# An interleave of two tensors: which part of each tensor makes up one tile, 4 MiB on end or the same 32 KiB of every partition

## The chip, the cores and the metric

The kernel runs on one core of one Trainium2 chip. The metric is the device time of one execution in microseconds (us). The time before the change is 314.18 us, the median of 3 runs (314.18 to 314.37).

## The reference

Two float32 tensors of 32 x 256 x 1024 elements (32 MiB each) are woven element by element into one of 32 x 256 x 2048 (64 MiB).

```python
batch, seq, dim = 32, 256, 1024
result = np.zeros((batch, seq, dim * 2), dtype=np.float32)
result[..., 0::2] = x
result[..., 1::2] = y
```

Seen flat, element i of x goes to place 2i and element i of y to place 2i + 1. So any cut of x and y into pieces at the same places gives pieces of the output that can be made apart from each other.

## The kernel before, in words

The flat tensors are cut into n = 8 tiles. A tile is 128 partitions x 8192 float32 (32 KiB of each partition, 4 MiB) of x and of y, and 128 x 16384 (64 KiB of each partition, 8 MiB) of the output. The helper `rows` makes the view of tile k: before the change it takes the k-th run of 4 MiB (8 MiB of the output) on end and gives each partition the next 32 KiB (64 KiB) of it. So rows that stand under each other in a tile's DMA start 32 KiB apart in x and y, and 64 KiB apart in the output.

In SBUF there are two buffers each for x (`xt`), y (`yt`) and the output (`ot`). An output buffer holds half a tile's output: 128 partitions x 8192 float32, 32 KiB a partition. Three queues work:

- SP issues all loads in order: x of tile 0 as two halves (lines 42 and 43), then for each tile x (line 50) and y (line 53). From tile 2 on it waits until VectorE has read the buffer that the load overwrites.
- VectorE (DVE) goes through tiles and halves. For each half, a copy puts 4096 elements of x in the even places of `ot` (line 67), and one puts 4096 of y in the odd places (line 70). From tile 1 on it waits before the first of them until the last store from that output buffer has landed.
- ACT issues the stores, each 4 MiB, when both copies of a half are done (line 83). The very first store is cut in two, of 8 KiB and of 24 KiB of each partition (lines 77 and 81).

Loads and stores are on queues of their own, q1 (loads, from SP) and q10 (stores, from ACT), and both are worked off by the same 16 DMA engines. The last of a DMA's 16 increments of its semaphore comes when all of its rows have landed. The first two loads are put ahead of a barrier at the program's start by the last lines of `tile_interleave_kernel`.

Of the kernel before, what the change touches and what calls it, by code (L numbers as in the profile page):

```python
# [3 lines left out]


def _interleave(nc, x, y, out):
    P = 128
    W = 8192
    H = W // 2  # L10

    total = 1
    for s in x.shape:
        total *= s
    n = total // (P * W)
    assert n * P * W == total

    def rows(ap, names, k):
        flat = ap.rearrange("b s d -> (b s d)")
        return flat[k * names : (k + 1) * names].rearrange("(p w) -> p w", p=P)  # L20

    fp32 = mybir.dt.float32
    xt = [nc.alloc_sbuf_tensor(f"xt{b}", [P, W], fp32).ap() for b in (0, 1)]
    yt = [nc.alloc_sbuf_tensor(f"yt{b}", [P, W], fp32).ap() for b in (0, 1)]
    ot = [nc.alloc_sbuf_tensor(f"ot{b}", [P, W], fp32).ap() for b in (0, 1)]

    xsem = [nc.alloc_semaphore(f"xsem{b}") for b in (0, 1)]
    hsem = nc.alloc_semaphore("hsem")
    qsem = nc.alloc_semaphore("qsem")
    ysem = [nc.alloc_semaphore(f"ysem{b}") for b in (0, 1)]  # L30
    woven = nc.alloc_semaphore("woven")
    osem = [nc.alloc_semaphore(f"osem{b}") for b in (0, 1)]


    cuts = [0, W // 4, W]
    parts = [slice(a, b) for a, b in zip(cuts, cuts[1:])]

    xs = [rows(x, P * W, k) for k in range(n)]
    ys = [rows(y, P * W, k) for k in range(n)]
    os_ = [rows(out, 2 * P * W, k) for k in range(n)]  # L40

    nc.sync.dma_start(out=xt[0][:, :H], in_=xs[0][:, :H]).then_inc(xsem[0], 16)
    nc.sync.dma_start(out=xt[0][:, H:], in_=xs[0][:, H:]).then_inc(hsem, 16)

    for k in range(n):
        b = k % 2
        if k >= 2:
            nc.sync.wait_ge(woven, 4 * (k - 2) + 3)
        if k:
            nc.sync.dma_start(out=xt[b], in_=xs[k]).then_inc(xsem[b], 16)  # L50
        if k >= 2:
            nc.sync.wait_ge(woven, 4 * (k - 2) + 4)
        nc.sync.dma_start(out=yt[b], in_=ys[k]).then_inc(ysem[b], 16)

    for k in range(n):
        b = k % 2
        for h in (0, 1):
            c = slice(h * H, (h + 1) * H)
            if h == 0:
                nc.vector.wait_ge(xsem[b], 16 * (k // 2 + 1))  # L60
            elif k == 0:
                nc.vector.wait_ge(hsem, 16)
            if k:
                nc.vector.wait_ge(osem[h], 16 * k)
            if (k, h) == (1, 0):
                nc.vector.wait_ge(qsem, 16)
            nc.vector.tensor_copy(out=ot[h][:, 0::2], in_=xt[b][:, c]).then_inc(woven, 1)  # L67
            if h == 0:
                nc.vector.wait_ge(ysem[b], 16 * (k // 2 + 1))
            nc.vector.tensor_copy(out=ot[h][:, 1::2], in_=yt[b][:, c]).then_inc(woven, 1)  # L70

    for k in range(n):
        for h in (0, 1):
            nc.scalar.wait_ge(woven, 4 * k + 2 * h + 2)
            if (k, h) == (0, 0):
                for c in parts[:-1]:
                    nc.scalar.dma_start(
                        out=os_[k][:, c], in_=ot[h][:, c]
                    ).then_inc(qsem, 16)
                c = parts[-1]  # L80
                nc.scalar.dma_start(out=os_[k][:, c], in_=ot[h][:, c]).then_inc(osem[h], 16)
                continue
            nc.scalar.dma_start(
                out=os_[k][:, h * W : (h + 1) * W], in_=ot[h]
            ).then_inc(osem[h], 16)

    nc.scalar.wait_ge(osem[0], 16 * n)
    used = sorted(s.num for s in [*xsem, hsem, qsem, *ysem, woven, osem[0]])
    assert used == list(range(used[0], used[-1] + 1)), used
    nc.scalar.sem_clear(range(used[0], used[-1] + 1))  # L90
    nc.sync.nop(nofuse=True).wait_op(osem[1], 16 * n, "sem-ge").then_inc(
        osem[1], -16 * n
    )


def kernel(tc, x, y, out):
    nc = tc.nc
    tc.close()
    tc.compile()

    _interleave(nc, x, y, out)

    blocks = nc.main_func.blocks
    for engine in (mybir.EngineType.SP, mybir.EngineType.SP):
        opening = blocks[0].instructions
        at, moved = next(
            (b, i)
            for b in blocks[1:]
            for i in b.instructions
            if i.engine == engine and i.opcode == "DMACopy"  # L110
        )
        assert not (moved.sync_info and moved.sync_info.on_wait)
        body = at.instructions
        body.remove(moved)
        gate = next(
            n
            for n, i in enumerate(opening)
            if i.engine == engine and i.opcode == "Drain"
        )
        opening.insert(gate, moved)  # L120
        at.instructions = body
        blocks[0].instructions = opening


# [1 line left out]
_INS = ['x', 'y']  # L126
_OUTS = [((32, 256, 2048), 'float32')]


# [23 lines left out]
```

## Time and profile before

| What | Value |
|---|---|
| Median of 3 runs | 314.18 us |
| Span of the profiled execution, first to last instruction | 312.9 us |
| Median less span: what lies around the span | 1.3 us |
| VectorE busy | 72.0 us of 312.9 |
| Moved between HBM and SBUF | 67.11 MB read, 67.11 MB written |
| Mean rate over the span | 429 GB/s |
| DMA packets | 4896 in 34 DMAs |
| From issue to landing, median: a store of 4 MiB | 34.1 us |
| From issue to landing, median: y, and x from tile 1 on | 41.5 and 24.3 us |

No total of its own is recorded for the profiled execution beside its span; the median of the runs stands in for it.

How to read it: the profile takes one execution. The DMA part lists each queue with the number of its packets, the MB it moved, and the time that its packets took as a share of 16 engines' span. 100% means that all 16 engines had a packet in hand all the time. The packets of a queue in a stretch, asked for by window, are counted by where they start, and one engine can begin a packet while another's end is still out, so the shares of a short stretch can add up to a little over 100%. Multiplying a share by 16 and by the length of the stretch gives engine time; divided by the MB moved, it is the engine time that one MB cost.

### The profile page before, as it was taken

The page shows a single profiled execution, that of the slowest core. Times are in us where ns is not written, and L with a number is a line of the kernel's source. Part 1 is how long each engine was busy: PE and PEld are TensorE (multiplying, and loading weights), DVE is VectorE, ACT ScalarE, POOL GpSimd, SP SyncE. Part 2 cuts the span into 40 slices and gives each one's busy share as a digit, 9 for nine tenths or more (in the row PEclk, how much of TensorE's full clock was granted, in tenths as well). Part 3 has the DMA queues.
Part 4 walks back from the last instruction along what each step waited for, and adds up shares of the span by engine and source line. Part 5 has one row for each costly group of instructions (what it writes and reads, how often), then busy time and mean ns, then how long its engine had stood idle before and what let it go on. Part 6 is the DMA issues. An engine that isn't in the chain of part 4 may idle for free.

```text
span 312.9 us, 114 instructions
## 1 busy us (share of the span) xinstructions
DVE 72.0 (23%) x32; POOL 0.2 (0%) x4
## 2 busy tenths in 40 slices
DVE  0216000501305023050220503205032050415410
POOL 0000000000000000000000000000000000000000
DMA  8999999999999999999999999999999999999998
GB/s 337 467 402 436 436 402 419 452 457 415 427 444 411 461 402 469 402 469 402 469 402 465 406 440 432 423 448 402 469 402 469 402 469 402 469 402 448 423 423 381
DMA packets 4896, 134.22 MB, mean 429 GB/s; under 512 B 544, under 2 KB 544, under 8 KB 544
## 3 DMA queue, kind: packets, MB, share of 16 engines
q1 hardware_dynamic: 2448, 67.11, 50.1%
q10 hardware_dynamic: 2448, 67.11, 49.7%
HBM read 67.11 MB, written 67.11 MB: 429 GB/s over the span
## 4 chain that ended last, share of the span: by engine, by line
DMA 82%; DVE 12%; issue 0%
DMA out_dram<-ot 76%; DMA yt<-in_y_dram 6%; DVE ot L70 6%; DVE ot L67 6%
## 5 line engine op out<-in xcount | busy, mean ns | idle before, releaser
L67 DVE COPY ot<-xt 128x4096 f32<-128x4096 f32 x16 | 36.7, 2295 | 213.8 <-DMA out_dram<-ot 206.5
L70 DVE COPY ot<-yt 128x4096 f32<-128x4096 f32 x16 | 36.6, 2288 | 12.3 <-DMA yt<-in_y_dram 12.3
L137 POOL MEMSET const-bfloat16-1.0<- 128x1 bf16 x1 | 0.1, 103 | 0.0
L137 POOL MEMSET const-uint8-127<- 128x1 uint8 x1 | 0.1, 102 | 0.0
L137 POOL MEMSET const-float32-0.0<- 128x1 f32 x1 | 0.1, 100 | 0.2 <-issue 0.2
L137 POOL MEMSET const-float32-1.0<- 128x1 f32 x1 | 0.1, 99 | 0.0
## 6 DMA issues: line engine op xcount, KB each, us to landing
out_dram<-ot ACTq DMA_DIRECT2D x15, 4096.0 KB, 34.1
yt<-in_y_dram SPq DMA_DIRECT2D x8, 4096.0 KB, 41.5
xt<-in_x_dram SPq DMA_DIRECT2D x7, 4096.0 KB, 24.3
xt<-in_x_dram SPq DMA_DIRECT2D x2, 2048.0 KB, 9.5
out_dram<-ot ACTq DMA_DIRECT2D x1, 3072.0 KB, 32.8
out_dram<-ot ACTq DMA_DIRECT2D x1, 1024.0 KB, 16.3
```

The costliest lines, as they stand in the source:

```text
L67: nc.vector.tensor_copy(out=ot[h][:, 0::2], in_=xt[b][:, c]).then_inc(woven, 1)
L70: nc.vector.tensor_copy(out=ot[h][:, 1::2], in_=yt[b][:, c]).then_inc(woven, 1)
L137: nc = _bacc.Bacc("TRN2", target_bir_lowering=False, num_devices=1)
```

## The change

One line of the helper `rows` changes. The flat tensor is first divided among the 128 partitions, so that each owns 256 KiB of x and of y (512 KiB of the output) on end, and tile k is the k-th 32 KiB (64 KiB) of each of them. Rows that stand under each other in a DMA now start 256 KiB apart in x and y, and 512 KiB apart in the output. The number of tiles, the DMAs, their sizes, the length of each row, the copies, the waits and their order stay as they are.

```diff
     def rows(ap, names, k):
         flat = ap.rearrange("b s d -> (b s d)")
-        return flat[k * names : (k + 1) * names].rearrange("(p w) -> p w", p=P)
+        return flat.rearrange("(p w) -> p w", p=P)[:, k * names // P : (k + 1) * names // P]
```

## The prediction

> **What bounds the kernel now.** I read the page's busy times first, then its DMA part, then the waits, then a table by stage.
>
> ```profile
> DVE 72.0 (23%) x32; POOL 0.2 (0%) x4
> DMA  8999999999999999999999999999999999999998
> DMA packets 4896, 134.22 MB, mean 429 GB/s; under 512 B 544, under 2 KB 544, under 8 KB 544
> q1 hardware_dynamic: 2448, 67.11, 50.1%
> q10 hardware_dynamic: 2448, 67.11, 49.7%
> ```
>
> VectorE works 23% of the span. The 16 DMA engines are busy in every slice; loads (q1) take 50.1% of their time and stores (q10) 49.7%, together 99.8%. So the span is the sum of all packets' times over 16: 0.998 x 312.9 = 312.3 us.
>
> ```profile
> DVE ot L67 <- DMA out_dram<-ot: 206.5, 14, 29.0
> ```
>
> In the waits, VectorE stands 206.5 us for stores. It has room to be late, the DMA engines have none.
>
> ```profile
> 0.00:28.60 28.60, 8.99 (x4) 0.20 (x4) 1.00 0.97 403
> 28.60:76.80 48.20, 4.50 (x3) 0.00 (x0) 1.00 1.02 435
> 76.80:270.40 193.60, 44.97 (x20) 0.00 (x0) 1.00 1.00 433
> 270.40:312.90 42.50, 13.49 (x6) 0.00 (x0) 1.00 0.97 419
> ```
>
> The table by stage (stretch, length, VectorE and GpSimd busy with counts, clock, DMA share, GB/s) shows the same in each stage: a share of 0.97 to 1.02. There is no stage in which a longer packet would be hidden.
>
> What does a packet cost? The DMA part of the steady stretch from 80 to 270 us, by queue: packets, MB, share.
>
> ```profile
> q1 hardware_dynamic: 1417, 41.19, 50.2%
> q10 hardware_dynamic: 1409, 41.16, 50.2%
> ```
>
> Loads: 0.502 x 16 x 190 us / 41.19 MB = 37.05 us of engine time per MB. Stores: 37.08. A row of 32 KiB (0.0328 MB) takes 1.21 us on its engine. Loads have rows 32 KiB apart, stores 64 KiB apart, and they cost the same within 0.1%: here it is the engine's own pace that sets a packet's time, and memory keeps up.
>
> It doesn't keep up everywhere. The same part for 0 to 7 us, where the first loads run alone:
>
> ```profile
> q1 hardware_dynamic: 160, 2.36, 87.6%
> ```
>
> This is 0.876 x 16 x 7 / 2.36 = 41.6 us per MB, 12% over the steady value. And for 25 to 42 us, where the first stores join the loads:
>
> ```profile
> q1 hardware_dynamic: 181, 5.41, 76.9%
> q10 hardware_dynamic: 160, 1.44, 20.0%
> ```
>
> Loads: 0.769 x 16 x 17 / 5.41 = 38.7, 4.3% over. So a packet can be stretched by what it meets in memory, by 0% in the steady state, by 4.3% and by 12% in two short stretches. Over the whole span the stretched loads cost (50.1% - 49.7%) x 312.9 = 1.25 us.
>
> **The change part by part.**
>
> *Instructions.* None is added, removed or moved: 32 copies of 2.29 us, 34 DMAs, the same waits. Copies work in SBUF alone, whose layout stays. Cost 0, and it needs no cover.
>
> *Issue.* The DRAM side of a load of x from tile 1 on, and of y, was one run of 4 MiB and becomes 128 rows with gaps. An issue of such a load takes 0.327 us on SP now; an issue of a store, whose rows have gaps already, takes 0.339 us on ACT. I cost it at 15 x 0.012 = 0.2 us of SP's time and nothing of the span: from tile 2 on SP sits idle for over 200 us before line 50 (218.1 us in 6 waits), and queued rows keep the engines busy meanwhile. If that cover were gone it would be 0.2 us.
>
> *Number of packets.* Both queues have 2448 packets for 67.11 MB, though before the change loads have one run and stores have gaps. So a packet already is a row (or an increment) in both cases, and the number stays. Cost 0.
>
> *The time of a packet.* This is the whole question. Rows go from 32 to 256 KiB apart (loads) and from 64 to 512 KiB (stores), so the rows that 16 engines work at in one moment are eight times as far apart. The trace before has no such distance, so I bound it. From below: all loads at the pace of the stores, the 1.25 us of stretched loads gone, 312.9 us. From the same side, the one comparison that the trace has (32 against 64 KiB) gives 0. From above: every packet stretched as the loads at 25 to 42 us are, 0.043 x 312.3 = 13.4 us, 327.6 us. The 12% of the first 7 us I don't carry over the whole run: that is a start from rest.
>
> Between 0 and 4.3% I take the middle, 2.15%, and on the stores alone, since their rows come to lie twice as far apart as the loads', the farthest from what the trace shows to be free. Stores take 0.497 x 312.9 = 155.5 us; 0.0215 x 155.5 = 3.3 us. The reason for taking more than the nearest row's 0: with 99.8% of the engines' time in use any stretch at all shows in full, and powers of two this large make many rows differ in few address bits. That is an inference from the layout, not a row.
>
> *The sum.* 0 + 0 + 0 + 3.3 us on a span of 312.9, so 316.2 us; with the 1.3 us by which the median of the runs (314.18) is over the span, **317.5 us**, 1.1% slower.
>
> The Trainium skill speaks against this change: its page "DMA: Bandwidth & Descriptors", section "Latency and other measured facts", lists copies of tiles of 128 rows of 16 KiB between HBM tensors, at 207 GB/s per direction with rows 512 KiB apart, against 214 in full, 164 at 2 MiB and 103 at 4 MiB, and advises laying tiles out contiguously. An estimate from that page, 214/207 on all packets, would make the sum 0.034 x 312.3 = 10.6 us, 324.8 us in all; on stores alone it would be 5.3 us, 319.5 us. The row from which I go, 64 KiB apart at 37.08 us per MB, lies outside what the page lists, and no trace so far shows 256 or 512 KiB.
>
> **The rivals.**
>
> *The engines' pace stays the bound (not slower).* Memory serves rows 256 and 512 KiB apart as fast as it serves 32 and 64; each packet of 32 KiB stays at 1.21 us. For it: two distances with the same cost, and the steady rate is the same with loads alone, both, or stores alone. Against it: the loads at 25 to 42 us, which show that memory can fall short. It decides as long as memory answers a row in less than 1.21 us. 314.2 us, chance 0.22.
>
> *The stretched loads of the opening go (faster).* The opening's 12% and 4.3% could come from rows that stand close together, and rows farther apart could spread better. It decides in the first 42 us only, and can give at most the 1.25 us above: 312.9 us; half of it, 313.6 us. Against it: the same close rows are read at full pace from 80 us on, so a start from rest explains the stretch as well. Chance 0.13.
>
> *Loads and stores both stretch, by 4.3% or more.* Rows meet in the same part of memory in every tile, both ways: 327.6 us if as at 25 to 42 us. For it: the engines work at their rows in step (equal packets, equal starts), so rows at equal distances stay at equal distances. Against it: the trace's only doubling costs nothing. Chance 0.20, for 321 us and more. This is what the page's rule would do here.
>
> *The change doesn't do what it says.* If the loads' gaps cut rows into more packets or left engines out, packets would number over 4896. The stores' rows with gaps give 2448 packets as the loads do, so I give this no chance of its own.
>
> **How the numbers follow.** Forecast (a mild stretch, 314.9 to 321 us, at 317.5): 0.45. Both directions: 0.20. No change: 0.22. Faster: 0.13. The likeliest case's own range is 314.9 to 321 us. The range that should hold 8 in 10 reaches below to 313.1 (the faster case but for its last part) and above to 326 (the case of both but for about half of it), leaving out some 0.13. A difference under 0.2% (0.6 us) is about what a measurement of this kernel can't tell from no change: slower 0.65, same 0.22, faster 0.13.
>
> **What would show it.** Right: the same 4896 packets; q10's share times 16 x span / 67.11 MB at 37.9 instead of 37.08 us per MB, q1's near 37.1 in the steady stretch; the wait of line 67 for stores longer by about the same 3 us; DMA still over 99%. Wrong: both queues at 37.05 to 37.1 in the steady stretch (the engines' pace stays the bound); q1 stretched more than q10 (it isn't the distance between rows that counts); a DMA share under 98% (then it is a wait, not a stretch); a gain that isn't in the first 42 us.

## The result and the profile after

The changed kernel takes **316.76 us** (median of 6 runs, 315.06 to 317.28), against 314.31 us before (6 runs, 314.18 to 314.37). The ratio is 1.0072, with a 95% interval of 1.0055 to 1.0089: slower by 2.45 us. The runs also scatter more, by 2.2 us instead of 0.2.

The DMA part of the page after, with the span in 40 slices:

```profile
span 315.4 us, 114 instructions
...
DMA  9999999999999999999999999999999999999996
...
DMA packets 4896, 134.22 MB, mean 426 GB/s; under 512 B 544, under 2 KB 544, under 8 KB 544
...
q1 hardware_dynamic: 2448, 67.11, 49.9%
q10 hardware_dynamic: 2448, 67.11, 49.3%
```

The packets are the same in number and size. Stores (q10) cost 0.493 x 16 x 315.4 / 67.11 = 37.07 us of engine time per MB: they didn't change at all. Loads (q1) went from 37.37 (worked out in the same way from the page before) to 37.52. Both queues together take 0.992 x 315.4 = 312.9 us, against 312.3 before. So longer packets explain 0.6 us (0.7 by the packet records, which aren't rounded as the shares are), and the span grew by 2.5. The other 1.9 us is time in which engines had nothing to do; the last slice, at 6 instead of 8, says where.

The stage at the end shows it. First before, then after, the last stretches by window (stretch, length, VectorE and GpSimd busy, clock, DMA share, GB/s); the last line of each is the last 2.5 us of the span:

```profile
305.00:310.40 5.40, 0.00 (x0) 0.00 (x0) 1.00 1.07 461
310.40:312.90 2.50, 0.00 (x0) 0.00 (x0) 1.00 0.49 210
```

```profile
305.00:312.90 7.90, 0.00 (x0) 0.00 (x0) 1.00 0.95 411
312.90:315.40 2.50, 0.00 (x0) 0.00 (x0) 1.00 0.06 26
```

The share is 0.49 before and 0.06 after. Both count packets by their start and leave out those begun earlier; by what lay inside the 2.5 us, the packet records give 0.80 before, where all engines end together, and 0.13 after, two engines of 16 on average. A few engines drag the end out. The packet records say the same: the 16 engines finish the last store within 0.24 us of each other before, and within 2.71 us after, where 12 are done within 0.52 us of the first and the other four need 1.50, 1.57, 1.83 and 2.71 us.

The records also show which packets made them late. Before, 49 loads of 32 KiB took over 1.25 us instead of 1.21, all in the first 55 us. After there are 78, of which 24 fall later, scattered up to 194 us into the span, up to 1.98 us long. No store of 32 KiB reaches 1.25 us in either. VectorE waits longer for stores in line 67:

```profile
DVE ot L67 <- DMA out_dram<-ot: 209.0, 14, 29.3
```

That is 2.5 us more than before.

### The profile page after: what moved, and what is told of

It is laid out like the page before. It is cut to its first block, busy times and chain, and to the rows that moved or that the text cites. A ratio compares the mean times of both kernels' runs of the same rounds, so it can differ in the third digit from the quotient of the medians.

```text
span 315.4 us, 114 instructions
## 1 busy us (share of the span) xinstructions
DVE 72.0 (23%) x32; POOL 0.2 (0%) x4
## 2 busy tenths in 40 slices
DMA packets 4896, 134.22 MB, mean 426 GB/s; under 512 B 544, under 2 KB 544, under 8 KB 544
## 3 DMA queue, kind: packets, MB, share of 16 engines
q1 hardware_dynamic: 2448, 67.11, 49.9%
q10 hardware_dynamic: 2448, 67.11, 49.3%
HBM read 67.11 MB, written 67.11 MB: 426 GB/s over the span
## 4 chain that ended last, share of the span: by engine, by line
DMA 82%; DVE 12%; issue 0%
DMA out_dram<-ot 76%; DMA yt<-in_y_dram 6%; DVE ot L70 6%; DVE ot L67 6%
```

## The experiments

Questions: do the loads take longer because of their own distance (theory L) or because of the stores' (theory S)? Is it aliasing, rows a large power of two apart (theory A), or the footprint, as each DMA now touches a whole tensor (theory F)? Each kernel is held against the kernel before, run on the same chip (314.20 to 314.24 us); ratios are given with their 95% intervals. Counts of long loads come from the packet records of the profiled execution of each kernel.

**One distance at a time.** The first two kernels choose the layout by tensor; `e2` has `ap is out` in the condition.

```diff
-        return flat.rearrange("(p w) -> p w", p=P)[:, k * names // P : (k + 1) * names // P]
+        if ap is not out:
+            return flat.rearrange("(p w) -> p w", p=P)[:, k * names // P : (k + 1) * names // P]
+        return flat[k * names : (k + 1) * names].rearrange("(p w) -> p w", p=P)
```

> Loads 256 KiB apart as after the change, stores 64 KiB apart as before it (the output's elements stand in other places, the work is the same). In the profile after, packets of stores kept their 1.21 us and some loads took longer, unevenly over the engines. Theory L (the loads' own distance stretches them): as after, 316 to 317.3 us, with scattered loads over 1.25 us and the engines' ends some 2 to 3 us apart. Theory S (stores 512 KiB apart crowd memory and the loads beside them wait): as before, 314.2 to 314.5 us, engines' ends 0.2 to 0.3 us apart. If both distances are needed: between, under 315.2.

> The mirror: loads 32 KiB apart, stores 512 KiB apart (output elsewhere placed). Theory L: as before, 314.2 to 314.5 us. Theory S: as after, 316 to 317.3 us, the loads stretched though their own rows are close. The prediction's step (stores stretch by their distance): q10 over 37.08 us per MB and about 317.5 us.

Measured: loads far alone 315.58 us, ratio 1.0037 (1.0022 to 1.0052); stores far alone 317.13 us, 1.0096 (1.0075 to 1.0118). The stores' distance alone does all that the change does (theory S), and the loads' alone does about half of it. Neither theory has it alone, and the two don't add up: with both it is 1.0072. With stores far, the page shows once more that it isn't the stores that are stretched:

```profile
q1 hardware_dynamic: 2448, 67.11, 49.9%
q10 hardware_dynamic: 2448, 67.11, 49.4%
```

At a span of 314.8 us, q10 costs 0.494 x 16 x 314.8 / 67.11 = 37.08 us per MB. The loads, whose own rows are as close as before the change, have 26 packets over 1.25 us after 55 us, and the last 2.5 us are as empty as after the change:

```profile
312.30:314.80 2.50, 0.00 (x0) 0.00 (x0) 1.00 0.06 26
```

With loads far alone there are only 6 of these packets; most of the engines' drift (how far they are out of step) comes in the first 55 us.

**Half the distance.**

```diff
+        g = 4
+        part = flat[k // g * g * names : (k // g + 1) * g * names]
+        return part.rearrange("(p w) -> p w", p=P)[:, k % g * names // P : (k % g + 1) * names // P]
```

> Half the distance of the change: groups of 4 tiles, loads 128 KiB and stores 256 KiB apart, right output. If the distance counts in proportion: some 315.3 us. If there is a threshold between this and the full distance (rows differ in higher address bits only): 314.2 to 314.5 us with no stretched loads after 50 us.

Measured: 314.27 us, ratio 1.0002 (0.9993 to 1.0010). Loads 128 KiB and stores 256 KiB apart cost nothing; no load over 1.25 us after 55 us, and the last 2.5 us are as full as before the change:

```profile
310.40:312.90 2.50, 0.00 (x0) 0.00 (x0) 1.00 0.49 210
```

The price doesn't grow in proportion to the distance: at half of it there is none. (This layout also halves the part of the tensor that one DMA touches; the next runs separate the two.)

**Distances that aren't powers of two.** First for the loads alone, then for both; the lines below are of the second kernel. It leaves out the eighth tile's place (in a shorter row there is no room for it) and uses the first's again; the last kernel is its control with the full powers of two.

```diff
+        step = names // P * 8 - 1024 * names // (P * W)
+        r = flat[: P * step].rearrange("(p w) -> p w", p=P)
+        c = k % (n - 1) * names // P
+        return r[:, c : c + names // P]
```

> The kernel after with loads 252 KiB apart instead of 256 (some elements read twice, some never), stores 512 KiB apart. If it is the power of two that makes rows meet (aliasing): 314.2 to 314.6 us, no scattered stretch. If it is being spread far over the tensor: 316 to 317.3 us as after. Under theory S with the stores' power of two alone: as after, too; e2 tells these two apart.

> As after, but rows 252 KiB (loads) and 504 KiB (stores) apart; the eighth tile takes the place of the first again, so the last part of each partition's share is left out, while as many bytes move. Theory A (aliasing: rows a large power of two apart meet in the same part of memory): the odd distances cure it, 314.2 to 314.6 us, no stretched loads after 55 us. Theory F (it is the footprint: each DMA touches the whole of a tensor, and something that has to be looked up per region of memory no longer fits): as after, 316 to 317.5 us.

> The control of the run with rows 252 and 504 KiB apart, which left the eighth tile's place out and used the first's again: the same, with rows 256 and 512 KiB apart. Theory A (the power of two does it): as after, 316 to 317.5 us. Theory F (seven eighths of the footprint was what helped there): 314.2 to 314.6 us.

Measured: 316.97 us, 1.0086 (1.0072 to 1.0099), for loads at 252 KiB with stores at 512; 314.33 us, 1.0006 (0.9997 to 1.0014), for 252 and 504 KiB; 317.31 us, 1.0109 (1.0088 to 1.0129), for the control. Curing the loads' distance alone doesn't help. With both cured nothing is lost that can be measured, and the seven eighths of the footprint do not explain it. Theory F falls, theory A stands, with one pair of odd distances tested. The profiled execution of the run at 252 and 504 KiB was the slowest of its eleven (315.16 us; the others 314.23 to 314.54), pulled apart mostly by loads in the opening; its trace has 4 loads over 1.25 us after 55 us against 24 after the change.

**Which rows meet.** Two layouts with the right output that keep one kind of neighbour close:

```diff
+        w = names // P
+        return flat.rearrange("(a k b w) -> k a b w", a=32, b=4, w=w)[k]
...
+        return flat.rearrange("(j k i w) -> k i j w", j=4, i=32, w=w)[k]
```

> Right output, other layout: 32 groups of 4 partitions; rows in a group stand next to each other (32 and 64 KiB), groups 1 MiB and 2 MiB apart. The footprint of each DMA is the whole tensor as after the change, and rows 4 partitions apart keep the distance that they have after it; only rows within a group come close. Theory F by regions of up to 2 MiB, and theory A between groups: as after, 316 to 317.3 us. Theory A between the rows within a group: 314.2 to 314.6 us.

> Right output, the reverse of the run with groups: partition 4i + j reads at j x 8 MiB + i x 32 KiB (stores: j x 16 MiB + i x 64 KiB). Rows 4 partitions apart are neighbours in memory, rows 1 partition apart lie in four far places; a DMA touches 4 stretches of 1 MiB (2 MiB). Theory F: small footprint in one DMA, 314.2 to 314.6 us. Theory A between rows 4 partitions apart: 314.2 to 314.6 us. Theory A between rows 1 partition apart, whatever engine has them: 316 us and more.

Measured: groups of four partitions close together and groups 1 and 2 MiB apart, 318.61 us, 1.0146 (1.0132 to 1.0161), the slowest of all and above the range that I had named; rows four partitions apart close together and the four of a group 8 and 16 MiB apart, 314.71 us, 1.0017 (1.0009 to 1.0026). So rows next to each other in a tile may lie 8 and 16 MiB apart at almost no cost, while groups of four that lie 1 and 2 MiB apart cost most. This fits rows of different groups meeting; it doesn't prove it, since the second layout also has only four far places in a DMA, the first 32. In the layout with groups 13 stores, too, took over 1.25 us (up to 1.51), all between 85 and 87 us. Most of the 0.5 us of the second layout has another source: a DMA with one more dimension takes 0.59 us to issue on SP instead of 0.37. The start of its timeline, and then of the kernel before:

```profile
0.00 0.59 SPq L43 DMA_DIRECT2D xt<-in_x_dram  x1
...
7.67 2.29 DVE L68 COPY ot<-xt 128x4096 f32<-128x4096 f32 x1 [7.67 <-DMA xt<-in_x_dram]
```

```profile
0.00 0.37 SPq L42 DMA_DIRECT2D xt<-in_x_dram  x1
...
7.33 2.30 DVE L67 COPY ot<-xt 128x4096 f32<-128x4096 f32 x1 [7.33 <-DMA xt<-in_x_dram]
```

The first data come 0.34 us later. The kernel with groups issues in the same way and has its first data 0.54 us later, at 7.87 us, so about 0.5 us of its 4.4 can be the opening.

**Twice through.** Does the drift of the engines end by itself, as the trace after suggested, where no load is stretched past 210 us?

```diff
+    m, n = n, 2 * n
...
-    xs = [rows(x, P * W, k) for k in range(n)]
+    xs = [rows(x, P * W, k % m) for k in range(n)]
```

(and the same for y and the output)

> The kernel after with its 8 tiles gone through twice (16 tiles, the second pass writes the same bytes again). At 38.7 us a tile in the steady part of before, before twice would take 314.2 + 309.8 = 624.0 us. If loads are stretched at random all along and the engines drift further apart: 2 x 2.5 us over, 629 us. If the drift ends the stretching (engines out of step no longer meet; in the trace after, no load is stretched past 210 us): 2.5 to 3 us over, 626.5 to 627 us.

> The kernel before with its 8 tiles gone through twice, to stand beside the kernel after gone through twice (631.51 us). At 38.73 us a tile: 314.2 + 309.8 = 624.0 us, with the engines' ends still 0.2 to 0.4 us apart. Theory (each beat of stretched loads is new, and nothing brings a late engine back): the second pass costs the layout after at least as much again as the first, so a difference of 5 us or more. Rival (before drifts as well in its second pass, so that the long run and not the layout counts): 627 us or more here.

Measured: 631.51 us after (626.67 to 633.71), 624.57 us before (624.46 to 624.85). The two ran on different chips, on which one pass of the kernel before took 314.24 and 314.21 us. The difference is 6.9 us, against 2.45 for one pass, and above both values that I had named (5 if the drift goes on, 2.5 to 3 if it ends the stretching). I had taken the quiet end of the one trace for a rule, and it was luck: in the long run loads are stretched to the end (276 over 1.25 us after 55 us, against 5 before). From 418 us on stores are stretched as well: 39 took over 1.25 us, up to 1.57, and none did in the kernel before gone through twice. That kernel ends with its engines 0.9 us apart, not 0.2 to 0.4; they come apart at 449 us, where a load of 1.75 us follows the one packet of a queue that the profile calls "instruction". The end, by window, after and then before:

```profile
580.00:630.90 50.90, 13.49 (x6) 0.00 (x0) 1.00 0.90 387
```

```profile
580.00:623.20 43.20, 13.49 (x6) 0.00 (x0) 1.00 0.96 413
```

By these shares, which leave out packets begun before 580 us, engines stand idle for (1 - 0.90) x 50.9 = 5.1 us of the end after, and 1.7 us before: 3.4 us of the 7.7 by which the two profiled spans differ. The rest is longer packets: the queues' shares on the two pages give 0.994 x 630.9 = 627.1 us after and 1.000 x 623.2 = 623.2 us before.

**Loads alone and stores alone, at the new distances.** The first leaves out the stores of seven tiles, the second the loads of seven tiles; both change the waits to match.

```diff
-    for k in range(n):
+    for k in (n - 1,):
         for h in (0, 1):
             nc.scalar.wait_ge(woven, 4 * k + 2 * h + 2)
```

```diff
-    for k in range(n):
+    for k in range(1):
         b = k % 2
         if k >= 2:
             nc.sync.wait_ge(woven, 4 * (k - 2) + 3)
```

> The kernel after without the stores of its first seven tiles: loads 256 KiB apart alone at the engines' full pace, the last tile is stored. Theory S (a load is stretched when it meets stores): no load over 1.25 us after the opening, loads at 37.06 us per MB, in all 1.4 + 155.4 us for the loads and some 30 us for the last tile's copies and stores. Theory L (the distance between the loads' own rows is enough): scattered stretched loads all along, 37.2 us per MB and over.

> The kernel after with the loads of its first tile alone; the other seven tiles store the same data. Stores 512 KiB apart alone at the engines' full pace. The prediction's step (stores 512 KiB apart are stretched): over 37.5 us per MB. Theory S in its form 'stores are taken up at full pace and the loads pay': 37.08 us per MB as before the change, engines' ends under 0.5 us apart. If stores at twice the rate in the mixed part overrun memory: stretched stores here, which would show that they were spared only by the loads between them.

Measured, one run each: 182.55 and 182.89 us (some 187 had been added up for the first). The queues in the steady part, loads alone from 12 to 150 us, then stores alone from 40 to 170 us:

```profile
q1 hardware_dynamic: 2046, 59.70, 100.4%
```

```profile
q10 hardware_dynamic: 1908, 55.71, 99.8%
```

That is 1.004 x 16 x 138 / 59.70 = 37.13 and 0.998 x 16 x 130 / 55.71 = 37.26 us per MB, 0.2% and 0.5% over the mixed steady state before. No load of 32 KiB is over 1.23 us in the first, and no store over 1.25 us in the second while it runs. The scattered long loads, of up to 1.98 us, don't appear here: they need loads and stores side by side. The hedge in the second expectation, stores stretched when they run at twice the rate, came out at 0.5%, spread evenly (1.219 us a packet of 32 KiB; the kernel before, whose stores lie 64 KiB apart, ends with stores alone at 1.213), with the engines' ends 0.2 us apart: no engine is left behind.

## Why the prediction was right in its number and wrong in its step

- **What bounds the kernel** held: every stretch of a packet shows, and so does an engine that falls behind. DMA is over 99% in use in both, and VectorE waits 2.5 us longer for stores (about 3 were forecast).
- **Instructions, issue and number of packets** at no cost held: 114 instructions, 4896 packets.
- **The time of a packet** is the step that failed. I put 2.15% on all stores, 3.3 us, "on the stores alone, since their rows come to lie twice as far apart". The stores' distance is indeed the stronger cause (317.13 us with it alone, 315.58 us with the loads'), but the stores weren't stretched: q10 stayed at 37.07 us per MB where 37.9 was forecast. The loads beside the stores are stretched, a few of them, by up to 0.77 us. The 2.15% was the middle between two bounds and came from no row.
- **The sum** assumed that a stretch spreads over 16 engines alike. Of the 2.5 us by which the span grew, 0.6 is the mean of longer packets (3.3 was forecast, on the stores; it came on the loads); 1.9 is how much farther the slowest engine ends behind the mean of the sixteen (2.1 us behind after, 0.1 before), for which my sum had no term. Total 3.3 against 2.45 measured: two errors of opposite sign, so that the number came out near was luck.
- **A sign that I named was wrong:** "q1 stretched more than q10 (it isn't the distance between rows that counts)". q1 was, and the distance counts all the same, as the run at half the distance and the one at 504 KiB show.
- **The rivals.** That the engines' pace stays the bound is true for stores and for all but a few loads, and would have been the whole truth at half the distance (314.27 us). Both directions stretched by 4.3% didn't come, and no gain in the opening: the loads over 1.25 us there are 49 before and 54 after. Nor does a start from rest, which I had held possible, explain them: before the change they begin at 25.9 us, after the issue of the first store (24.2 us) and before its first packet (28.6 us), and in the run with loads alone no load of 32 KiB is over 1.23 us. What stretches them stays open.
- **The Trainium skill**, page "DMA: Bandwidth & Descriptors", section "Latency and other measured facts", has the kind of effect and the cure right: large powers of two between rows cost rate, and a pad of a few KiB on the row pitch restores it; here 4 and 8 KiB less restore it too (314.33 us). Its size doesn't carry over: 207 to 214 GB/s would be 3.4% on all packets, and the whole kernel lost 0.72%. That page's reason, channels of memory that rows moving in step share, is called an inference there; these runs agree with it and don't prove it.

What stays open: why loads pay for the distance of the stores' rows, and stores only in the long run and in the layout with groups; whether the late engines are the same in each run, since the records that I read don't name an engine; and which distances besides 512 KiB (stores) and 256 KiB (loads) cost: 504 with 252 KiB doesn't, nor does 256 with 128.

## What to carry to other kernels

Where the DMA engines are the bound, count not only the mean time of a packet but the slowest engine: compare the sum of the queues' shares with the span, and look at the DMA share in the last few microseconds. Where loads and stores run side by side, don't let the rows of one DMA lie a large power of two apart (here 512 KiB for stores, and to a lesser degree 256 KiB for loads); a pitch a few KiB off, or a tile from half the distance, cost nothing here. Loads may be stretched by a layout that only the stores have: try each direction by itself.

## What the runs showed of the hardware that I had not expected

- Sixteen engines that work at their own pace stay within 0.2 to 0.3 us of each other through 280 us, if nothing stretches a packet. An engine that has fallen behind hardly catches up: in the kernel before gone through twice the completions of one DMA lie 1.02 us apart at 453 us and still 0.88 at the end. With 16 tiles the difference between the layouts is 6.9 us, not twice 2.45.
- In one pass a store's packet keeps 1.21 us beside loads that take up to 1.98 us; loads alone and stores alone at the same distances show no such packets. In two passes stores of up to 1.57 us appear as well.
- The layout with 128 KiB (256 KiB) in one piece per group of four partitions is slower (318.61 us) than the one with every row by itself (316.76 us): longer pieces don't help if the pieces lie 1 and 2 MiB apart. (The 256 KiB of the output are in one piece by tile; a single store takes every other 32 KiB of it.)
